# Modulation of the K blocks in four chunks due at their first K tile, the gate root's chain kept together on VectorE, and the first product of a block by operand parts, in a two-layer GLA/FoX trunk

## Chip, cores and metric

One core of a Trainium2 chip. The metric is the device time of one execution of the whole program in microseconds (us), median of three runs. One execution was also profiled; times inside the kernel come from its trace.

## The reference, cut to what matters

A two-layer decoder trunk on one sequence of 256 tokens and 2048 features, in float32. Every sub-layer is normalised, then scaled and shifted by columns that come from a conditioning vector `c`:

```python
mod = c_act @ w_mod[l] + b_mod[l]            # 6 sections of 2048: shift, scale, gate, twice
h = rmsnorm(x, norm_mix[l]) * (1 + scale_m) + shift_m
x = x + gate_m * mixer(h)                    # layer 0: GLA, layer 1: FoX
h = rmsnorm(x, norm_ffn[l]) * (1 + scale_f) + shift_f
x = x + gate_f * conv_ffn(h)

# GLA mixer
proj = h @ w_in                              # 2048 x 6160: q, k (1024 each), v, r (2048 each), a (16)
log_alpha = log_sigmoid(a @ w_gate + b_gate) / 16
o = chunked_linear_attention(q, k, v, log_alpha)
o = rmsnorm(o, g_norm) * silu(r)             # the norm is over each head of 512 columns
return o @ w_out
```

`c_act` is the activated conditioning vector. The tolerance asks for nearly full float32 products.

## The kernel before, in words

**Products.** Activations stand transposed (features on the 128 partitions, tokens along the free dimension), so the input of a projection is 16 K tiles of 128 features x 256 tokens. Each float32 operand is split into a high part and a rest. A weight tile of 128x1024 is cast on ScalarE to `wh` (line 125) and its rest `wl = w - wh` is formed on VectorE (line 129). A product then is three matmuls for each 128 columns, high x high (line 621), high x rest (line 622), rest x high (line 623), so 24 matmuls with 256 moving columns for one weight tile. In this text such a weight tile with its 24 matmuls is a **use**; they are numbered in the order in which their loads are issued, use 1 being the first tile of `q`. `wh` and `wl` each have four buffers, taken in turn, so the cast for use n+4 waits for the last matmul of use n.

**K blocks.** The first projection (GLA's `w_in`) doesn't wait for all of `h`. Its 16 K tiles are cut into three blocks, `BLOCKS = (4, 5, 7)`: K tiles 0 to 3, 4 to 8, 9 to 15. In a block the sections q, k, v0, v1, r0, r1 are swept in turn (one use for each K tile), then the 16 narrow columns `a`; in the last block `a` stands behind q. Block 1 is uses 1 to 24 and 25 (`a`), block 2 uses 26 to 55 and 56 (`a`), block 3 uses 57 to 63 (q), 64 (`a`) and 65 to 99. Sums of earlier blocks are copied back into PSUM by ScalarE (line 609). From use 100 on `w_out` follows.

**Modulation.** The columns `sc_m` and `sh_m` of K tiles 0 to 3 (the head) are made at the start on TensorE: eight early loads of 1 MB of `w_mod` and eight sums of eight matmuls (line 1270), with five filling matmuls behind some of them (line 1308, `KEEP = 5`). Those of the other K tiles are accumulated on VectorE by outer products: a step loads two tiles of 128 rows of `w_mod` in one DMA and does a scalar-times-tensor addition for each (line 273 for the first of a section, then line 275) on a tile `acc` as wide as the block has columns: 640 columns for block 2, 896 for block 3, 32 additions for each. When a section's last step is through, VectorE transposes and reduces `acc` into `red` (lines 285 and 286), TensorE closes the sum over partitions with a 128x20 or 128x28 matmul (line 302), and VectorE adds the bias and writes the columns (lines 318, 322). `tick()`, called at each use, hands out these steps at a pace; before the first use of a block a hook (`hooks[end - 1] = drain_bg`) does all that is left. Later sections (for the gate of layer 0 and for the FFN) are accumulated in the same manner with 1024 columns.

**h.** `make_h` makes for each K tile `hn = x * r` (line 527, VectorE), `h hi` with scale and shift (line 528, ScalarE), the same once more in float32 (line 530 on VectorE for K tiles 0 to 2 of a projection, else line 532 on ScalarE), and the rest `h lo` (line 533, VectorE).

**GLA's gate norm.** For each pair of heads `rsqrt` (lines 403 to 416) forms 1/sqrt by a start value and Newton steps: 13 small VectorE instructions on 128x4 numbers, each reading what the one before wrote. Its result is spread by a diagonal `dg` (line 422) and a TensorE matmul with ones (line 424).

**Order.** Each engine executes its own list of instructions strictly in the order in which a scheduler has put them when the kernel is built; `issue_after` gives it an additional edge. What stands on VectorE in one list is thus `wl`, `acc`, the reductions, `h`, the chain of the gate norm and more. SyncE issues all weight loads, also in order.

## Time and profile before

| | |
|---|---|
| device time, median of 3 runs | 2445.64 us (2445.29 to 2446.72) |
| the profiled execution's own time | 2444.97 us |
| its span in the trace | 2443.3 us |
| TensorE busy (matmuls) | 2388.1 us, 98% |
| VectorE busy | 1901.7 us, 78% |
| ScalarE busy | 1326.6 us, 54% |
| HBM read over the span | 260 GB/s |

Busy times are of the trace; matmuls are pipelined, so the busy time of one matmul (0.28 us in the rows) is longer than the distance between the starts of two. "a <- b" behind an idle time says that the instruction waited for the event b. `PEclk` is the TensorE clock as a share of full speed.

### The profile page before, as it was taken

Reading aid. Unit: us, or ns where it says so; the run is one execution under the profiler, and the core shown is the slowest. Engines: PE = TensorE matmul, PEld = TensorE weight load, DVE = VectorE, ACT = ScalarE, POOL = GpSimd, SP = SyncE. Lnnn points to the kernel's source line nnn. Section 1 sums busy time; section 2 is a strip of 40 time slices with the busy share of each in tenths; the row PEclk is TensorE's granted clock in tenths of the full one; section 3 lists DMA queues with packets and bytes.
Section 4 is the critical chain, followed back from the end, with each engine's and each line's share of the span. In section 5 each row is a group of like instructions: output and inputs, shape, how many; then the busy total and the mean of one; then the engine's idle time right before and its main releaser. Section 6 shows DMA issues by size and latency. Waiting matters only on the chain.

```text
span 2443.3 us, 46907 instructions
## 1 busy us (share of the span) xinstructions
PE 2388.1 (98%) x19089; PEld 2292.1 (94%) x19093; DVE 1901.7 (78%) x2548; ACT 1326.6 (54%) x1819; POOL 16.1 (1%) x35
## 2 busy tenths in 40 slices
PE   7999998999999999999999999999999999999998
PEld 5898898999999999999988888999999999999998
DVE  5887878887689999987577998887776777777544
ACT  4666864544656556543464555554755555555433
POOL 0000000000000000000000000000000000000000
PEclk9999998999999999999999999999999999999999
DMA  9997877899668999899589887686777777756553
GB/s 377 328 338 240 288 249 274 288 322 322 181 191 278 314 302 313 315 327 322 168 291 314 298 288 244 210 300 234 232 232 234 234 233 235 232 193 220 192 190 104
DMA packets 188293, 638.31 MB, mean 261 GB/s; under 512 B 23849, under 2 KB 24859, under 8 KB 187692
## 3 DMA queue, kind: packets, MB, share of 16 engines
q1 hardware_dynamic: 187112, 634.12, 77.2%
q8 instruction: 149, 2.44, 0.4%
q10 hardware_dynamic: 964, 1.20, 0.1%
q14 instruction: 68, 0.56, 0.1%
HBM read 633.14 MB, written 2.10 MB: 260 GB/s over the span
## 4 chain that ended last, share of the span: by engine, by line
PE 95%; DVE 2%; ACT 2%; DMA 1%; issue 1%; SPq 0%; DVEq 0%; ACTq 0%
PE pa L622 25%; PE pa L623 25%; PE pa L621 25%; PE pa L668 5%; PE pa L669 5%; PE pa L667 5%; DVE wl L129 1%; DMA wm<-in_w_mod_dram 1%; PE pe L1270 0%; DVE acc L275 0%; ACT wh L125 0%; PE pm L483 0%; PE pm L877 0%; DMA xtok<-in_x_dram 0%; PE pm L1088 0%
## 5 line engine op out<-in xcount | busy, mean ns | idle before, releaser
L125 ACT CAST wh<-w 128x1024 fp32r<-128x1024 f32 x820 | 857.4, 1048 | 965.7 <-PE pa L622 735.3
L129 DVE TENSOR_TENSOR wl<-w,wh 128x1024 fp32r<-128x1024 f32 x820 | 996.5, 1217 | 438.8 <-ACT wh L125 428.6
L622 PE MATMUL pa<-h,wh 128*128 128x256 f32 x3584 | 993.7, 278 | 13.3 <-DVE h L533 13.3
L621 PE MATMUL pa<-h,wh 128*128 128x256 f32 x3584 | 991.6, 278 | 2.2 <-ACT h L528 1.3
L623 PE MATMUL pa<-h,wl 128*128 128x256 f32 x3584 | 991.0, 278 | 1.7 <-DVE wl L129 1.7
L622 PEld LDWEIGHTS pa<-h,wh 128*128 128x128 f32 x3584 | 677.4, 189 | 15.1 <-DVE h L533 14.8
L621 PEld LDWEIGHTS pa<-h,wh 128*128 128x128 f32 x3584 | 675.3, 189 | 5.4 <-issue 1.5
L623 PEld LDWEIGHTS pa<-h,wl 128*128 128x128 f32 x3584 | 675.6, 189 | 2.0 <-DVE wl L129 1.9
L622 PE MATMUL pa<-op,wh 128*128 128x256 f32 x1920 | 529.4, 277 | 1.8 <-DVE op L549 1.8
L621 PE MATMUL pa<-op,wh 128*128 128x256 f32 x1920 | 528.9, 278 | 0.4 <-ACT op L548 0.2
L623 PE MATMUL pa<-op,wl 128*128 128x256 f32 x1920 | 524.8, 277 | 0.0
L275 DVE SCALAR_TENSOR_TENSOR acc<-wm,cT,acc 128x1024 f32<-128x1024 f32 (+2 forms) x360 | 444.3, 1235 | 10.7 <-DMA wm<-in_w_mod_dram 9.4
L622 PEld LDWEIGHTS pa<-op,wh 128*128 128x128 f32 x1920 | 362.0, 189 | 2.3 <-DVE op L549 2.3
L621 PEld LDWEIGHTS pa<-op,wh 128*128 128x128 f32 x1920 | 361.2, 189 | 1.1 <-ACT r L750 0.6
L623 PEld LDWEIGHTS pa<-op,wl 128*128 128x128 f32 x1920 | 359.2, 189 | 0.0
L668 PE MATMUL pa<-wh,h 128*128 128x512 f32 x512 | 200.2, 392 | 0.0
L667 PE MATMUL pa<-wh,h 128*128 128x512 f32 x512 | 198.8, 391 | 0.0
L669 PE MATMUL pa<-wl,h 128*128 128x512 f32 x512 | 194.4, 392 | 0.0
L669 PEld LDWEIGHTS pa<-wl,h 128*128 128x128 f32 x512 | 96.0, 188 | 19.7 <-DVE wl L129 0.3
L667 PEld LDWEIGHTS pa<-wh,h 128*128 128x128 f32 x512 | 96.1, 188 | 19.4
L668 PEld LDWEIGHTS pa<-wh,h 128*128 128x128 f32 x512 | 96.1, 188 | 19.2
L1140 ACT ACTIVATE y<-u,cw 128x256 f32<-128x256 f32 x176 | 101.6, 599 | 6.7 <-DVE act L1156 4.1
(264 smaller groups left out, 1351.3 us busy)
## 6 DMA issues: line engine op xcount, KB each, us to landing
wm<-in_w_mod_dram SPq DMA_DIRECT2D x320, 512.0 KB, 5.2
w<-in_ffn_w_up_dram SPq DMA_DIRECT2D x320, 512.0 KB, 4.5
w<-in_ffn_w_down_dram SPq DMA_DIRECT2D x176, 512.0 KB, 4.5
w<-in_fox_w_in_dram SPq DMA_DIRECT2D x128, 512.0 KB, 5.1
w<-in_gla_w_in_dram SPq DMA_DIRECT2D x96, 512.0 KB, 5.8
w<-in_gla_w_out_dram SPq DMA_DIRECT2D x32, 512.0 KB, 5.9
w<-in_ffn_w_up_dram SPq DMA_DIRECT2D x64, 256.0 KB, 4.0
w<-in_fox_w_out_dram SPq DMA_DIRECT2D x32, 512.0 KB, 5.9
```

The costliest lines, as they stand in the source:

```text
L125: nc.scalar.copy(out=hi, in_=src)
L129: order["v"] = nc.vector.tensor_tensor(out=lo, in0=src, in1=hi.bitcast(F32), op=ALU.subtract).ins
L275: nc.vector.scalar_tensor_tensor(out=st["a"], in0=wt[:, j, :], scalar=col, in1=st["a"], op0=ALU.mult, op1=ALU.add)
L621: nc.tensor.matmul(o, wh[:, ms], rh, start=(first and m % 2 == 0), stop=False, skip_group_check=True)
L622: nc.tensor.matmul(o, wh[:, ms], rl, start=False, stop=False, skip_group_check=True)
L623: nc.tensor.matmul(o, wl[:, ms], rh, start=False, stop=last, skip_group_check=True)
L667: nc.tensor.matmul(o, lh[:, ts_], wh[:, hs_], start=first, stop=False, skip_group_check=True)
L668: nc.tensor.matmul(o, ll[:, ts_], wh[:, hs_], start=False, stop=False, skip_group_check=True)
L669: nc.tensor.matmul(o, lh[:, ts_], wl[:, hs_], start=False, stop=last, skip_group_check=True)
L1140: nc.scalar.activation(y, u, AF.Identity, scale=cw[:, l * 3 + 2, r:r + 1], bias=cw[:, 6 + l, r:r + 1])
```

## The change

1. **Chunks.** The modulation of K tiles 4 to 15 is queued at the first use in four chunks, `MARKS = (4, 7, 9, 13, 16)`: K tiles 4-6, 7-8, 9-12, 13-15, that is 384, 256, 512 and 384 columns, each for scale and for shift. A step is now four tiles of 128 rows of `w_mod` (eight for 256 columns) in one DMA, with an addition for each; the DMAs are 28 instead of 32, of the same bytes in all, with rows of 1 to 2 KB instead of 2.5 and 3.5. All steps are handed out at one pace over block 1 and 2; if a chunk isn't complete when `h` asks for its first K tile, the rest is done there and its closing matmul comes at once (`flush_resting(True)`).
2. **Start.** The first three of the eight early sums stand ahead of the token sum on TensorE; three fillers instead of five; K tile 0's `h` comes ahead of the second and third weight split.
3. **Chain.** Each `wl`, and each `acc` addition but a section's first, is put behind the last instruction of the newest `rsqrt` chain (as of the last `tick`), so that the chain's 13 instructions stand together. `scale_of(0)` and `normalise(0)`, `normalise(1)` are queued earlier, and the paces of the side work and of the steps behind it change.
4. **First product of a block by operand parts.** The first weight tile that meets a fresh `h` does all high x high matmuls first, then all high x rest, then all rest x high.
5. The second modulation is on VectorE for the first four K tiles behind each of 0, 4, 9 in layer 0's mixer, and for the first five of every other `h`. The look-ahead of the weight loads is 2 until use 50 instead of 20; `SLOAD` is 100 instead of 48.

```diff
-NEAR = 20
+NEAR = 50
-KEEP = 5
+KEEP = 3
+MARKS = (4, 7, 9, 13, 16)
+EARLY = 3
-BG0, BG1 = 0.95, 0.75
+BG0, BG1 = 0.95, 0.95
...
             if after is not None:
                 es.enter_context(tc.issue_after(after))
+            es.enter_context(behind_chain())
             order["v"] = nc.vector.tensor_tensor(out=lo, in0=src, in1=hi.bitcast(F32), op=ALU.subtract).ins
...
-                        nc.vector.scalar_tensor_tensor(out=st["a"], in0=wt[:, j, :], scalar=col, in1=st["a"],
-                                                       op0=ALU.mult, op1=ALU.add)
+                        with behind_chain():
+                            nc.vector.scalar_tensor_tensor(out=st["a"], in0=wt[:, j, :], scalar=col, in1=st["a"],
+                                                           op0=ALU.mult, op1=ALU.add)
...
+    def behind_chain():
+        return tc.issue_after(chain["on"]) if chain["on"] is not None else ExitStack()
...
-            if m < 3:
-                nc.vector.tensor_scalar(out=t, in0=t, scalar1=sc, scalar2=sh, op0=ALU.mult, op1=ALU.add)
-            else:
-                nc.scalar.activation(t, t, AF.Identity, scale=sc, bias=sh)
+                if m - (max(b for b in STARTS if b <= m) if (l, kind) == (0, "m") else 1) < 4:
+                    nc.vector.tensor_scalar(out=t, in0=t, scalar1=sc, scalar2=sh, op0=ALU.mult, op1=ALU.add)
+                else:
+                    nc.scalar.activation(t, t, AF.Identity, scale=sc, bias=sh)
...
+        def by_part(ms, args):
+            edge = None
+            for n_ in range(3):
+                with ExitStack() as es:
+                    if edge is not None:
+                        es.enter_context(tc.issue_after(edge))
+                    for m in ms:
+                        last_ = mms(m, *args, n_)
+                    edge = last_
...
-        side.extend((apply(0), scores(2), apply(1), scores(3)))
+        side.extend((apply(0), scores(2), apply(1), scores(3), scale_of(0)))
         fold("v1", piece("v1", kts, off["v1"]))
         drain_side()
-        side.extend((apply(2), apply(3), scale_of(0), scale_of(2), normalise(0), normalise(1), normalise(2), normalise(3)))
+        side.extend((normalise(0), normalise(1), apply(2), apply(3), scale_of(2), normalise(2), normalise(3)))
...
     def staged_h(m):
-        if m in STARTS[:-2]:
-            n_ = STARTS.index(m) + 1
-            for key in ("sc_m", "sh_m"):
-                queue(mod_tasks(0, key, STARTS[n_] * P, BLOCKS[n_] * P, wide=True))
-            n_use = 6 * BLOCKS[n_ - 1]
-            set_pace(n_use - EASE)
-            end = fetched["use"] + n_use + (m > 0)
-            hooks[end - 1] = drain_bg
-            hooks[end] = lambda: h(STARTS[n_])
+        if m == 0:
+            for m0, m1 in zip(MARKS, MARKS[1:]):
+                for key in ("sc_m", "sh_m"):
+                    queue(mod_tasks(0, key, m0 * P, (m1 - m0) * P, wide=True))
+                need[m0] = len(bg)
+            pace["bg"] = len(bg) / float(6 * MARKS[2] + 2)
+            use = 6 * MARKS[0]
+            hooks[use] = lambda: h(MARKS[0])
+            hooks[use + 3] = lambda: h(MARKS[1])
+            use = 6 * MARKS[2] + 1
+            hooks[use] = lambda: h(MARKS[2])
+            hooks[use + 4] = lambda: h(MARKS[3])
+        if m in need:
+            while steps_done[0] < need[m]:
+                bg_step()
+            flush_resting(True)
         return first_h(m)
```

What this does to the lists of the engines is shown at three places. The first is VectorE where block 1 ends; before, `wl_1026` is the rest of `a` (use 25), `wl_1065` and `wl_1101` those of uses 26 and 27, and `acc_733` the second section of block 2:

```order
L275 SCALAR_TENSOR_TENSOR acc_733<-wm_875,cT,acc_733 128x640 x2
L129 TENSOR_TENSOR wl_996<-w_943,wh_995 128x1024
L129 TENSOR_TENSOR wl_1026<-w_984,wh_1025 128x176
L275 SCALAR_TENSOR_TENSOR acc_733<-wm_939,cT,acc_733 128x640 x2
L129 TENSOR_TENSOR wl_1065<-w_987,wh_1064 128x1024
L285 STREAM_TRANSPOSE mt_1056<-acc_733 128x512
L285 STREAM_TRANSPOSE mt_1059<-acc_733 128x128
L286 TENSOR_REDUCE red_1055<-mt_1056 128x16
L286 TENSOR_REDUCE red_1055<-mt_1059 128x4
L129 TENSOR_TENSOR wl_1101<-w_989,wh_1100 128x1024
L318 TENSOR_TENSOR mod<-pm_1092,bm 32x5 x4
```

The same place after; `wl_1184` is the rest of use 28, `wl_1213` that of use 29, and `acc_908` and `acc_1070` are scale and shift of K tiles 7 and 8:

```order
L132 TENSOR_TENSOR wl_1184<-w_1111,wh_1183 128x1024
L279 SCALAR_TENSOR_TENSOR acc_1070<-wm_870,cT,acc_1070 128x256
L290 TENSOR_REDUCE red_987<-mt_988 128x8
L279 SCALAR_TENSOR_TENSOR acc_1070<-wm_870,cT,acc_1070 128x256
L279 SCALAR_TENSOR_TENSOR acc_1070<-wm_947,cT,acc_1070 128x256
L322 TENSOR_TENSOR mod<-pm_1063,bm 32x2 x4
L279 SCALAR_TENSOR_TENSOR acc_1070<-wm_947,cT,acc_1070 128x256
L326 SCALAR_TENSOR_TENSOR mod<-mod,vec 128x2
L279 SCALAR_TENSOR_TENSOR acc_1070<-wm_947,cT,acc_1070 128x256 x6
L289 STREAM_TRANSPOSE mt_1150<-acc_1070 128x256
L290 TENSOR_REDUCE red_1149<-mt_1150 128x8
L132 TENSOR_TENSOR wl_1213<-w_1181,wh_1212 128x1024
```

The last two additions of block 2's sections stood two uses ahead of the boundary; now ten of the narrower ones stand behind the rest of use 28, inside block 2. On TensorE the matmul that reads `red_1149` stands behind the 72 products of uses 26 to 28 and ahead of `a` (use 25), which before came first.

The second place is VectorE where block 2 ends. Before, `acc_1675` is the second section of block 3, `wl_2061` and `wl_2097` the rests of uses 57 and 58:

```order
L129 TENSOR_TENSOR wl_2022<-w_1850,wh_2021 128x192
L275 SCALAR_TENSOR_TENSOR acc_1675<-wm_1846,cT,acc_1675 128x896
L590 MEMSET w_2144 128x112
L275 SCALAR_TENSOR_TENSOR acc_1675<-wm_1881,cT,acc_1675 128x896
L129 TENSOR_TENSOR wl_2061<-w_1883,wh_2060 128x1024
L275 SCALAR_TENSOR_TENSOR acc_1675<-wm_1881,cT,acc_1675 128x896
L129 TENSOR_TENSOR wl_2097<-w_1915,wh_2096 128x1024
L285 STREAM_TRANSPOSE mt_2052<-acc_1675 128x512
L285 STREAM_TRANSPOSE mt_2055<-acc_1675 128x384
L286 TENSOR_REDUCE red_2051<-mt_2052 128x16
L286 TENSOR_REDUCE red_2051<-mt_2055 128x12
```

After, `acc_2035` is the shift of K tiles 13 to 15, `wl_2384` and `wl_2417` the rests of uses 63 and 64, and `acc_2358` the next section, of 1024 columns:

```order
L132 TENSOR_TENSOR wl_2384<-w_2160,wh_2383 128x1024
L276 TENSOR_SCALAR acc_2358<-wm_2254,cT 128x1024
L279 SCALAR_TENSOR_TENSOR acc_2035<-wm_1999,cT,acc_2035 128x384
L132 TENSOR_TENSOR wl_2417<-w_2214,wh_2416 128x224
L279 SCALAR_TENSOR_TENSOR acc_2358<-wm_2256,cT,acc_2358 128x1024
L279 SCALAR_TENSOR_TENSOR acc_2035<-wm_2094,cT,acc_2035 128x384 x4
L279 SCALAR_TENSOR_TENSOR acc_2358<-wm_2356,cT,acc_2358 128x1024
L289 STREAM_TRANSPOSE mt_2323<-acc_2035 128x384
L290 TENSOR_REDUCE red_2322<-mt_2323 128x12
L322 TENSOR_TENSOR mod<-pm_2360,bm 32x3 x4
```

Six additions now stand between the rest of use 64 and the reduction. On TensorE the matmul that reads `red_2322` stands directly behind use 60.

The third place is VectorE at the second chain of the gate norm. Before (lines 410 to 416 are the chain's, `wl_4111` and `wl_4215` rests of uses 108 and 111):

```order
L414 TENSOR_TENSOR grs<-rt_3530,grs 128x4
L275 SCALAR_TENSOR_TENSOR acc_3700<-wm_3992,cT,acc_3700 128x1024
L129 TENSOR_TENSOR wl_4111<-w_3926,wh_4110 128x1024
L410 TENSOR_TENSOR rt_3530<-rv_3529,grs 128x4
L275 SCALAR_TENSOR_TENSOR acc_3700<-wm_4031,cT,acc_3700 128x1024
L129 TENSOR_TENSOR wl_4147<-w_3962,wh_4146 128x1024
L411 TENSOR_TENSOR rt_3530<-rt_3530,grs 128x4
L275 SCALAR_TENSOR_TENSOR acc_3700<-wm_4067,cT,acc_3700 128x1024
L129 TENSOR_TENSOR wl_4180<-w_4001,wh_4179 128x1024
L416 SCALAR_TENSOR_TENSOR grs<-rt_3530,grs 128x4
...
L422 TENSOR_SCALAR dg_3703<-ident,grs 128x128
```

After, at the second chain (`wl_3733` is the rest of use 96, `pm_3625` the closing matmul of the squares on TensorE):

```order
L964 COPY pvar<-pm_3625 128x2
L415 TENSOR_SCALAR rv_3662<-pvar 128x4
...
L422 TENSOR_TENSOR rt_3663<-rv_3662,grs 128x4
L423 TENSOR_TENSOR rt_3663<-rt_3663,grs 128x4
L428 SCALAR_TENSOR_TENSOR grs<-rt_3663,grs 128x4
L279 SCALAR_TENSOR_TENSOR acc_2992<-wm_3602,cT,acc_2992 128x1024
L132 TENSOR_TENSOR wl_3733<-w_3474,wh_3732 128x1024
L435 TENSOR_SCALAR dg_3711<-ident,grs 128x128
```

The chain's 13 instructions stand together, and the next `acc` addition and the next `wl` behind them. The first chain stands in the same way between `pvar<-pm_3257` ahead of it and `acc` and the rest of use 88 behind it.

More of the change, by code (lines that the diff above doesn't have):

```diff
@@ L94 @@
     cnt = [0]
-    order = {"v": None, "f": None}
+    order = {"v": None, "f": None, "w": None}
     def nm(s):
@@ L363, in tick @@
     def tick():
-        prefetch(PEND)
+        prefetch(min(PEND, fetched["use"] // 2 + 1))
+        chain["on"] = chain["new"]
         flush_resting()
@@ L434, in fetch_x, with load_x @@
         return xs
-    def load_x(xs):
+    def load_x(xs, between):
         for m in range(0, KT, 2):
@@ L445, in load_x @@
         half_sum()
-        token_sum(ss["t"][:, 0, :], True, True)
+        with tc.issue_after(between()):
+            token_sum(ss["t"][:, 0, :], True, True)
     ss = {}
@@ L620, in mms @@
             o = ps[m // 2][:, m % 2, :]
-            nc.tensor.matmul(o, wh[:, ms], rh, start=(first and m % 2 == 0), stop=False, skip_group_check=True)
-            nc.tensor.matmul(o, wh[:, ms], rl, start=False, stop=False, skip_group_check=True)
-            nc.tensor.matmul(o, wl[:, ms], rh, start=False, stop=last, skip_group_check=True)
+            for i, (w_, r_) in enumerate(((wh, rh), (wh, rl), (wl, rh))):
+                if n_ is None or n_ == i:
+                    mm = nc.tensor.matmul(o, w_[:, ms], r_, start=(first and i == 0 and m % 2 == 0),
+                                          stop=last and i == 2, skip_group_check=True)
+            return mm.ins
+        def by_part(ms, args):
+            edge = None
+            for n_ in range(3):
+                with ExitStack() as es:
+                    if edge is not None:
[3 more added lines that the diff above has]
+                    edge = last_
         for k in kts:
@@ L640, in stream_a @@
                         mms(m, *args)
+            elif fresh["h"]:
+                fresh["h"] = False
+                by_part(range(8), (k, wh, wl, rh, rl))
             else:
@@ L1292, with first_sums @@
         early_load(*args)
-    load_x(xs)
+    def first_sums():
+        with tc.issue_after(order["x"]):
+            for args in todo[:EARLY]:
+                last_ = early_sum(*args)
+        return last_
+    load_x(xs, first_sums)
     with tc.issue_after(order["s"]):
```

47 lines of the change are left out of this document (36 added, 11 removed).

## The prediction

> **What bounds the kernel now.** First the page's busy times and the chain of waits that ended last.
>
> ```profile
> PE 2388.1 (98%) x19089; PEld 2292.1 (94%) x19093; DVE 1901.7 (78%) x2548; ACT 1326.6 (54%) x1819; POOL 16.1 (1%) x35
> PE 95%; DVE 2%; ACT 2%; DMA 1%; issue 1%; SPq 0%; DVEq 0%; ACTq 0%
> ```
>
> TensorE (PE) sets the time nearly everywhere. So only two things count: what PE waits for, and how long it runs at a lower clock behind a wait. PE's waits, from the view of waits:
>
> ```profile
> PE pa L622 <- DVE h L533: 13.3, 7, 5.4
> PE pm L424 <- DVE dg L422: 8.3, 1, 8.3
> PE pm L483 <- DVE ss L476: 4.0, 1, 4.0
> PE pa L623 <- DVE wl L129: 1.7, 1, 1.7
> PE pm L302 <- DVE red L286: 1.7, 1, 1.7
> ```
>
> The change works on these. The windows around them (columns: time, busy time and instructions of PE, of the weight loads, of VectorE, ScalarE, GpSimd, then PE's clock, DMA share, GB/s):
>
> ```profile
> 100.00:110.00 10.00, 10.00 (x90) 10.00 (x90) 9.21 (x15) 4.62 (x7) 0.00 (x0) 1.00 0.69 209
> 110.00:120.00 10.00, 4.58 (x26) 4.26 (x25) 5.76 (x13) 9.97 (x20) 0.00 (x0) 0.78 1.00 380
> 120.00:130.00 10.00, 10.00 (x80) 10.00 (x80) 6.46 (x9) 3.66 (x4) 0.00 (x0) 0.88 0.68 214
> 200.00:210.00 10.00, 5.54 (x36) 5.05 (x35) 7.12 (x14) 9.49 (x18) 0.23 (x2) 0.83 0.38 107
> 210.00:220.00 10.00, 10.00 (x74) 10.00 (x75) 7.21 (x13) 5.82 (x10) 0.00 (x0) 0.83 0.40 112
> 380.00:390.00 10.00, 4.08 (x37) 3.89 (x35) 8.89 (x12) 2.10 (x2) 0.00 (x0) 0.93 1.03 410
> 390.00:400.00 10.00, 5.74 (x22) 4.86 (x23) 7.09 (x13) 3.78 (x18) 0.00 (x0) 0.50 0.55 213
> 400.00:410.00 10.00, 10.00 (x66) 10.00 (x66) 6.46 (x11) 3.33 (x4) 0.00 (x0) 0.72 0.26 77
> ```
>
> Undisturbed, PE does 90 matmuls in 10 us. What a window lacks of 90 is lost time, waits and low clock together: boundary 1 (110 to 130) 64 + 10 = 74 matmuls, 8.2 us; boundary 2 (200 to 220) 54 + 16 = 70, 7.8 us; the gate norm (380 to 410) 53 + 68 + 24 = 145, 16.1 us, of which I take off 2.5 for slower small matmuls that are in it anyway (estimate): 13.6. That is all the change could win there.
>
> What a use costs each engine, from the groups by form between 42 and 420 us, two casts that wait for PE, and PE's matmuls at the low clock:
>
> ```profile
> 106.70 1.05 ACT L125 CAST wh<-w 128x1024 fp32r<-128x1024 f32 x1 [1.67 <-PE pa L622]
> 109.42 1.05 ACT L125 CAST wh<-w 128x1024 fp32r<-128x1024 f32 x1 [1.67 <-PE pa L622]
> L129 DVE TENSOR_TENSOR wl<-w,wh 128x1024 fp32r<-128x1024 f32 x113 | 137.3, 1221 | 47.3 <-ACT wh L125 42.4 <-PE pm L424 3.2 <-PE pa L623 1.1
> L275 DVE SCALAR_TENSOR_TENSOR acc<-wm,cT,acc 128x1024 f32<-128x1024 f32 x47 | 60.1, 1278 | 7.4 <-DMA wm<-in_w_mod_dram 7.1
> L275 DVE SCALAR_TENSOR_TENSOR acc<-wm,cT,acc 128x896 f32<-128x896 f32 x30 | 34.3, 1142 | 0.2
> L275 DVE SCALAR_TENSOR_TENSOR acc<-wm,cT,acc 128x640 f32<-128x640 f32 x30 | 26.3, 880 | 0.4
> L129 DVE TENSOR_TENSOR wl<-w,wh 128x224 fp32r<-128x224 f32 x1 | 0.4, 386 | 0.0
> L285 DVE STREAM_TRANSPOSE mt<-acc 128x384 f32<-128x384 f32 x2 | 1.1, 538 | 0.0
> L286 DVE TENSOR_REDUCE red<-mt 128x12 f32<-128x384 f32 x2 | 1.1, 542 | 0.0
> 120.13 0.41 PE L621 MATMUL pa<-h,wh 128*128 128x256 f32 x1
> 120.34 0.41 PE L622 MATMUL pa<-h,wh 128*128 128x256 f32 x1
> ```
>
> A use is 2.72 us of PE (109.42 - 106.70). An addition costs 0.880 us at 640 columns, 1.278 at 1024: 0.22 us and 1.04 us for each 1000 columns. So 384 columns are 0.61 us, 256 are 0.48, 512 are 0.75 (worked out, not in the trace). At the low clock matmuls start every 0.21 us (120.34 - 120.13) instead of every 0.11 (10 us through 90). The clock columns 0.78 and 0.88 of the windows at boundary 1 mean some 6.8 us at half clock (2 x 10 x 0.22 + 2 x 10 x 0.12); PE works in 5.2 of them and so loses 2.6. I use that for each stall.
>
> **The change part by part.** *Start.*
>
> ```profile
> 2.19 17.25 SPq L248 DMA_DIRECT2D wm<-in_w_mod_dram  x8
> wm<-in_w_mod_dram SPq DMA_DIRECT2D x8, 1024.0 KB, 11.2
> 34.56 1.06 PE L1270 MATMUL pe<-wm,cz 128*32 128x512 f32 x8
> 38.07 1.58 ACT L528 ACTIVATE h<-hn,mod 128x256 fp32r<-128x256 f32 x3
> 38.72 0.74 PE L621 MATMUL pa<-h,wh 128*128 128x256 f32 x4 [1.34 <-ACT h L528]
> ```
>
> The eighth early load is issued by 19.44 us and lands some 11.2 later, 30.6; its sum begins only at 34.56, because PE does the token sum (a wait of 4.0 us), fillers and seven other sums first. With three sums ahead of the token sum and fewer fillers the last sum ends at about 31.7 at best, limited by the load. That is 35.62 - 31.7 = 3.9 us; `h` ahead of a cast of 1.05 us gives up to 1 more, of which I count 0.6: **-4.5 us** (bounds -5.5 and, if the load lands later because three more tiles are asked for, -1.5).
>
> *Boundary 1.* What PE waited for at 111.5 (h lo, 5.4 us) is gone, since K tiles 4 to 6 are ready before. But K tiles 7 and 8 are due three uses later, and their last ten 256-column additions stand behind the rest of use 28, whose cast waits for the end of use 24 (four buffers). From there: cast 1.05, `wl` 1.22, ten additions 4.8, a transpose and two reductions of 256 columns 1.2 (estimated from those of 384), small writes 0.8, in all some 9.1 us, less what the starts overlap (0.4). PE has 72 products in that time, 8.2 us: it waits 0.5 to 0.9 at the closing matmul. What is queued behind that matmul on PE is everything, `a` and all of uses 29 on. Then comes `a`, and use 29's cast waits for its end: three casts of 1.05 stand one behind the other before PE's next product (use 31's), 3.2 us; two `wl` later cost 1.6 and 1.3 more (the `aT` copy, an `hn` and 512-column additions lie between). If VectorE comes to use 24 with a lead of only 62.5 us of work against 65.3 of PE, uses 26 and 28 wait up to 3 us as well. The waits are 6.6 to 7, or some 10 with the poor lead; with the low clock behind that is 9.3 to 12.6, and I take 11.5, nearer to the poor lead, because VectorE has 20 us more to do in these blocks (next part): against 8.2 **+3.3** (bounds 0 and +5).
>
> *Block 2.* The work on VectorE up to use 56's rest, summed by its rows and these durations, is 160.8 us after use 1's rest, before 140.5:
>
> ```profile
> 40.81:109.00 68.19, 66.92 (x472) 63.14 (x473) 61.70 (x79) 36.40 (x48) 0.00 (x0) 0.95 0.94 346
> 109.00:203.00 94.00, 87.06 (x621) 81.81 (x619) 78.79 (x94) 63.63 (x95) 0.00 (x0) 0.96 0.89 318
> ```
>
> VectorE was busy 61.70 + 78.79 = 140.5 of 162 us. 128 additions in place of 64 pay the 0.22 us of each twice (14 us); the rest are second modulations moved from ScalarE and further small writes. The DMAs are 28 for 32 on SP's queue, the bytes the same. From use 30 to 54 that is 71.5 us against 24 x 2.72 = 65.3 of PE, so VectorE, which had room, is level with PE or behind. I count 0 here and take the lateness where it ends, at boundary 2; bounds 0 and +5.
>
> *Boundary 2.* The closing matmul that reads the last chunk's `red` stands on PE directly behind use 60. On VectorE the reduction stands behind use 64's rest, which waits for use 60's buffers, and six additions: 0.39 (224 columns wide, by its group) + 1.28 + 4 x 0.61 + 1.28 + 0.54 + 0.54 = 6.5 us in which PE has nothing. Then four small writes, h hi and h lo for K tile 13, some 0.65 + 0.6 + 0.9 and the ways between the engines, of which `a`'s 12 matmuls (1.4 us) cover the half: 1.4 more (estimate). Low clock behind: 2.6. Sum 10.5 against 7.8: **+2.7** (bounds -2, if use 64's rest is there earlier, and +5).
>
> *Gate norm.* The two chains in the trace, the first one's first and last instruction and two of the second's last four:
>
> ```profile
> 329.91 0.17 DVE L403 TENSOR_SCALAR rv<-pvar 128x4 f32<-128x4 f32 x1
> 333.72 0.16 DVE L416 SCALAR_TENSOR_TENSOR grs<-rt,grs 128x4 f32<-128x4 f32 x1
> 382.44 0.15 DVE L411 TENSOR_TENSOR rt<-rt,grs 128x4 f32<-128x4 f32 x1
> 391.81 0.15 DVE L416 SCALAR_TENSOR_TENSOR grs<-rt,grs 128x4 f32<-128x4 f32 x1
> ```
>
> The first ran nearly unbroken (3.97 us from the first start to the last end with one `wl` of 1.22 inside, so 2.8 alone) and cost PE nothing. The second was drawn out by `wl` and `acc` and cost 8.3. Now both stand together, and with that both stand, 2.8 us, an addition of 1.28 and 1.22, **ahead of the rest that PE needs next**: 5.3 us for use 88 and as much for use 96, counted from the closing matmul of the squares on PE, less the small score products beside it (1.8 at use 88, none at use 96): 3.5 and 5.3. The matmuls that read the squares wait for VectorE too: 1.0 + 2.2 at the first, 0.9 at the second. Low clock behind each, 2.6 twice. Sum 18.1 against 13.6: **+4.5** (bounds -6, if the first chain costs as little as before and only the second counts, and +6). Elsewhere (first products by parts in later sublayers, five second modulations on VectorE, FoX's chains) I take **-0.5** (bounds -4 and +3): the waits for h lo beyond boundaries 1 and 2 are 13.3 - 5.4 - 2.8 = 5.1 us at most, of the row of L533 above and this one:
>
> ```profile
> 209.88 0.39 PE L622 MATMUL pa<-h,wh 128*128 128x256 f32 x1 [2.78 <-DVE h L533]
> 203.16 0.41 PE L302 MATMUL pm<-red,quad 128*128 128x28 f32 x2 [1.68 <-DVE red L286]
> 204.32 0.41 PE L692 MATMUL pm<-h,wh 128*128 128x256 f32 x1
> ```
>
> Sum: -4.5 + 3.3 + 2.7 + 4.5 - 0.5 = +5.5. The profiled execution took 2444.97 us, 0.7 under the median; from the median 2445.64 it is 2451.1.
>
> The last two rows are also the ground for the low clock: a wait of 1.68 us, and 1.2 us later matmuls take 0.41. The Trainium skill, "TensorE: Matmul & The Clock Gate", section "Part 1: The HAM clock gate", says that the clock halves after at least one idle window of about 3.4 us of PE. The trace has it behind half of that; by the rule the sum would be +0.3 instead of +5.5 (rivals, below), and I go by the rows.
>
> **The rivals.** *The stalls go* (faster). VectorE runs ahead, so that the sums and chains are through before PE comes to them. For it: VectorE is idle a fifth of the time, and before, the first chain cost nothing. Against it: the order of rows and four buffers. It decides at use 60 and use 88: if the closing matmul there waits under 2 us, boundary 1 costs 4, boundary 2 costs 3 and the gate 7 instead of 8.2, 7.8 and 13.6, so -15.6 - 4.5 - 0.5 = -20.6: 2425. *Short waits leave the clock up.* The stalls at boundary 1 and at use 88 are made up of single waits of 3.5 us and less. Without 2.6 us behind each of the two the sum is +0.3: 2446, no change. The row at 204.32 speaks against. The Trainium skill's section named above would have it so. *The loads come late* (slower still). The look-ahead of 2 goes on until use 50, and the chunks' loads have rows of 1 to 2 KB where 2.5 and 3.5 stood. In block 1 the DMA share is 0.94 at 346 GB/s; if PE waits 0.3 us at each of 30 uses: +9 on the sum, 2460. *It doesn't do what it says*: the list shows the chains together and the chunks in place, so I give that nothing.
>
> **How the numbers follow.** Forecast 0.56, the stalls go 0.28, clock stays up 0.08, late loads 0.08. 0.2% of this kernel, 4.9 us, is about what a measurement can tell from no change. Inside the forecast the bounds reach from about -4 to +14, so of 0.56 I put 0.38 over +4.9, 0.16 within, 0.02 below. Faster: 0.28 + 0.02 = 0.30; same 0.16 + 0.08 = 0.24; slower 0.38 + 0.08 = 0.46. The forecast's own range is 2442 to 2460. The range for 8 in 10 reaches into the first rival: 2430 to 2461.
>
> **What would show it.** Right: the first product before 35 us; a PE wait for `red` of about 6.5 us near 200 us; waits for `wl` of 3 us and more at both chains; VectorE busy over 90% between use 30 and 60. Wrong: no wait over 2 us between 100 and 220 us, or PE's clock full through 300 to 400.

## The result and the profile after

| | before | changed |
|---|---|---|
| device time, median | 2445.47 us (2442.87 to 2446.72, 4 runs) | 2457.06 us (2456.01 to 2459.43, 4 runs) |
| ratio to before, 95% interval | | 1.0050 [1.0033, 1.0068] |
| profiled execution, its span | 2444.97, 2443.3 us | 2457.0, 2455.3 us |

The changed kernel is slower by 11.6 us, 0.5%; 2451 had been forecast, with a range of 2430 to 2461. First the page's busy times and the view of PE's waits, after (columns: total, times, longest; lines 650 and 717 are the products, 306 the closing matmul of a modulation section, 497 a token sum, 963 the matmul that reads the gate norm's squares):

```profile
PE 2388.3 (97%) x19095; PEld 2288.8 (93%) x19095; DVE 1921.5 (78%) x2645; ACT 1314.1 (54%) x1804; POOL 19.6 (1%) x35
PE pa L650 <- DVE wl L132: 13.5, 8, 5.2
PE pm L306 <- DVE red L290: 9.6, 2, 8.3
PE pa L650 <- DVE h L551: 4.9, 3, 2.3
PE pa L717 <- DVE wl L132: 4.3, 3, 2.4
PE pm L497 <- DVE ss L490: 4.0, 2, 2.7
PE pm L963 <- DVE gsq L960: 2.8, 2, 2.0
PE pm L437 <- DVE dg L435: 0.5, 1, 0.5
```

PE's busy time is as before (2388.1). Its large old waits have shrunk: h lo from 13.3 to 4.9 us, `dg` from 8.3 to 0.5. In their place stand waits for weight rests (1.7 before, 17.8 now) and for `red` (1.7 before, 9.6 now): VectorE is waited for in both kernels, for another product of its list. Behind 31 us no wait of PE is for a load and only one, of 0.5 us, for a cast, so the rival "the loads come late" did not come.

To see where the 12.0 us of span come from, take moments that both traces have, each an instruction that runs when PE has come to a certain place. Before (the cast that waits for the end of use 24 stands at 109.42 in a row above; then the first of GLA's gate columns, the first residual of `w_out`, the FFN's norm, the first operand of layer 1's output product):

```profile
248.09 1.23 DVE L722 SCALAR_TENSOR_TENSOR la<-la,le 128x1024 f32<-128x1024 f32 x1
463.37 0.88 DVE L700 SCALAR_TENSOR_TENSOR xT<-pa,mod,xT 128x256 f32<-128x256 f32 x2 [0.87 <-PE pa L623]
471.14 0.42 DVE L494 SCALAR_TENSOR_TENSOR ra<-pm,rb 128x256 f32<-128x256 f32 x1 [1.79 <-ACT rb L492]
1567.84 0.69 DVE L549 TENSOR_TENSOR op<-oTf,op 128x512 fp32r<-128x512 f32 x1 [0.61 <-ACT op L548]
```

The same after:

```profile
105.35 1.05 ACT L127 CAST wh<-w 128x1024 fp32r<-128x1024 f32 x1 [2.30 <-PE pa L650]
252.26 1.22 DVE L770 SCALAR_TENSOR_TENSOR la<-la,le 128x1024 f32<-128x1024 f32 x1
468.19 0.48 DVE L748 SCALAR_TENSOR_TENSOR xT<-pa,mod,xT 128x256 f32<-128x256 f32 x1 [0.31 <-PE pa L650]
478.91 0.42 DVE L508 SCALAR_TENSOR_TENSOR ra<-pm,rb 128x256 f32<-128x256 f32 x1 [4.71 <-ACT rb L506]
1579.86 0.69 DVE L575 TENSOR_TENSOR op<-oTf,op 128x512 fp32r<-128x512 f32 x1 [0.61 <-ACT op L574]
```

The differences are -4.1, +4.2, +4.8, +7.8 and +12.0 us. So the start gains 4.1 up to the end of use 24, the K blocks lose 8.3 behind that, the gate norm 0.6, the way from `w_out` into the FFN 3.0, and layer 1's mixer 4.2; nothing behind it differs.

Now the windows of the changed kernel at the places of the forecast (columns as in the prediction):

```profile
100.00:110.00 10.00, 7.78 (x63) 7.19 (x62) 10.00 (x23) 4.02 (x5) 0.00 (x0) 1.00 0.27 107
110.00:120.00 10.00, 6.84 (x58) 6.44 (x56) 9.61 (x25) 6.09 (x10) 0.00 (x0) 1.00 0.51 178
120.00:130.00 10.00, 7.61 (x60) 7.00 (x60) 9.85 (x19) 3.58 (x5) 0.00 (x0) 1.00 0.66 243
210.00:220.00 10.00, 4.63 (x41) 4.43 (x40) 9.72 (x14) 2.09 (x3) 0.00 (x0) 0.92 0.90 304
220.00:230.00 10.00, 7.10 (x39) 7.13 (x40) 4.23 (x10) 3.06 (x6) 0.23 (x2) 0.57 0.46 167
320.00:330.00 10.00, 7.97 (x96) 7.52 (x98) 3.94 (x19) 3.05 (x7) 0.64 (x3) 0.88 0.01 2
330.00:340.00 10.00, 7.99 (x74) 7.81 (x73) 9.94 (x13) 2.58 (x3) 0.43 (x1) 0.95 0.71 241
360.00:370.00 10.00, 4.83 (x34) 4.75 (x33) 7.92 (x23) 4.81 (x8) 0.00 (x0) 0.76 0.22 69
```

At boundary 1 VectorE is busy 29.5 of 30 us (10.00 + 9.61 + 9.85), and PE lacks 27 + 32 + 30 = 89 matmuls of 270, 9.9 us (8.2 before). At boundary 2 it lacks 49 + 51 = 100, 11.1 us (7.8 before). At the gate norm VectorE is idle 6 us of 320 to 330 and the loads stand nearly still (2 GB/s): the edges hold additions and rests back until the first chain has run, up to 330 us. The rows of the second chain show the same pattern; below them are PE's waits at the two chains:

```profile
362.65 0.17 DVE L415 TENSOR_SCALAR rv<-pvar 128x4 f32<-128x4 f32 x1
365.04 0.16 DVE L428 SCALAR_TENSOR_TENSOR grs<-rt,grs 128x4 f32<-128x4 f32 x1
365.12 1.28 DVE L279 SCALAR_TENSOR_TENSOR acc<-wm,cT,acc 128x1024 f32<-128x1024 f32 x1
366.31 1.22 DVE L132 TENSOR_TENSOR wl<-w,wh 128x1024 fp32r<-128x1024 f32 x1
```

```profile
332.52 0.39 PE L650 MATMUL pa<-h,wl 128*128 128x256 f32 x1 [2.01 <-DVE wl L132]
367.58 0.58 PE L650 MATMUL pa<-h,wl 128*128 128x256 f32 x1 [5.17 <-DVE wl L132]
```

The second chain takes 2.55 us together; the addition and the rest of use 96 follow, and PE's product begins 0.05 us after that rest ends, having waited 5.17 us.

### The profile page after: what moved, and what is told of

Same layout as the page of the kernel before. It is cut to its first block, busy times and chain, and to the rows that moved or that the text cites. A ratio compares the mean times of both kernels' runs of the same rounds, so it can differ in the third digit from the quotient of the medians.

```text
span 2455.3 us, 46997 instructions
## 1 busy us (share of the span) xinstructions
PE 2388.3 (97%) x19095; PEld 2288.8 (93%) x19095; DVE 1921.5 (78%) x2645; ACT 1314.1 (54%) x1804; POOL 19.6 (1%) x35
## 4 chain that ended last, share of the span: by engine, by line
issue 47%; PE 45%; DVE 4%; DMA 2%; ACT 1%; POOL 0%; SPq 0%; DVEq 0%; POOLq 0%; ACTq 0%
PE pa L650 39%; DVE acc L279 1%; DMA wm<-in_w_mod_dram 1%; DVE wl L132 1%; PE pa L717 1%; PE pa L715 1%; PE pa L716 1%; DMA w<-in_gla_w_in_dram 1%; ACT wh L127 0%; PE pm L1136 0%; PE pm L925 0%; DMA xtok<-in_x_dram 0%; PE pm L1100 0%; PE pm L1099 0%; PE pm L1127 0%
## 5 line engine op out<-in xcount | busy, mean ns | idle before, releaser
L650 PE MATMUL pa<-h,wh 128*128 128x256 f32 x7168 | 1230.5, 278 | 6.8 <-DVE h L551 4.9
L650 PEld LDWEIGHTS pa<-h,wh 128*128 128x128 f32 x7168 | 1079.4, 189 | 11.2 <-DVE h L551 5.7
L650 PE MATMUL pa<-h,wl 128*128 128x256 f32 x3584 | 975.7, 278 | 13.6 <-DVE wl L132 13.5
L650 PE MATMUL pa<-op,wh 128*128 128x256 f32 x3840 | 651.1, 276 | 0.7 <-ACT wh L127 0.5
L650 PEld LDWEIGHTS pa<-op,wh 128*128 128x128 f32 x3840 | 573.1, 188 | 1.1 <-ACT wh L127 0.7
L279 DVE SCALAR_TENSOR_TENSOR acc<-wm,cT,acc 128x1024 f32<-128x1024 f32 (+3 forms) x420 | 456.4, 1089 | 4.0 <-DMA wm<-in_w_mod_dram 2.1
L1191 DVE SCALAR_TENSOR_TENSOR y<-u,cw,y 128x254 f32<-128x254 f32 x176 | 83.1, 479 | 2.8
L1189 DVE SCALAR_TENSOR_TENSOR y<-u,cw,y 128x255 f32<-128x255 f32 x176 | 84.0, 477 | 0.0
L1210 ACT COPY u<-pa 128x512 f32<-128x512 f32 x88 | 49.8, 581 | 0.7
L542 ACT ACTIVATE h<-hn,mod 128x256 fp32r<-128x256 f32 x64 | 35.2, 594 | 14.0 <-DVE mod L322 9.5
## 6 DMA issues: line engine op xcount, KB each, us to landing
wm<-in_w_mod_dram SPq DMA_DIRECT2D x20, 1024.0 KB, 11.1
```

Source lines behind the costliest of these rows:

```text
L279: nc.vector.scalar_tensor_tensor(out=st["a"], in0=wt[:, j, :], scalar=col, in1=st["a"], op0=ALU.mult, op1=ALU.add)
L542: hot = nc.scalar.activation(hi, t, AF.Identity, scale=sc, bias=sh).ins
L650: mm = nc.tensor.matmul(o, w_[:, ms], r_, start=(first and i == 0 and m % 2 == 0), stop=last and i == 2, skip_group_check=True)
L1189: nc.vector.scalar_tensor_tensor(out=y[:, 1:], in0=u[:, :T - 1], scalar=cw[:, l * 3 + 1, r:r + 1], in1=y[:, 1:], op0=ALU.mult, op1=ALU.add)
L1191: nc.vector.scalar_tensor_tensor(out=y[:, 2:], in0=u[:, :T - 2], scalar=cw[:, l * 3, r:r + 1], in1=y[:, 2:], op0=ALU.mult, op1=ALU.add)
L1210: nc.scalar.copy(out=u[:, 2 * b:2 * b + 2, :], in_=ps[b])
```

## Experiments

All were timed beside runs of the kernel before on the same chip; the ratio is to those. The number that counts is the ratio, since the median of before moved between 2446.0 and 2446.6 us (2445.5 beside the changed kernel), so differences of medians across groups of runs can be off by about 1 us. Three groups: parts taken out of the change, parts put into the kernel before, and parts taken out of the best combination.

**Without the edges behind the chains** (1):

```diff
     def behind_chain():
-        return tc.issue_after(chain["on"]) if chain["on"] is not None else ExitStack()
+        return ExitStack()
```

> The changed kernel without the edges that put each weight rest and each addition behind the newest chain; all else is kept. Theory (edges): they are the cause of the new waits at both chains of the gate norm, of the wait for a weight rest of 2.4 us in layer 1's mixer, and, since the stalled additions hold up the loads behind them, of the late token sum ahead of layer 0's FFN (2.7 us). Then layer 1's mixer gives back about 4 us and the FFN's start 3 to 5; the gate norm comes back to a second chain that is drawn out, about as dear as now (plus or minus 3). In all 2449 us, 2445 to 2453. Rival (work): those losses come from the additional second modulations on VectorE and the higher pace of the additions; then the edges don't matter outside the gate norm, and the time is 2455 to 2459.

Measured: 2439.3 us, ratio 0.9975 [0.9964, 0.9985]: 17.8 us under the changed kernel and faster than before. The edges theory holds, by more than it said (its interval began at 2445). One part of it did not come: the second chain is not drawn out again, it takes 5.4 us here (367.88 to 373.25 us) and PE doesn't wait for `dg`. In layer 1's mixer PE is busy throughout again; the chain begins at 1458.32 us here, and PE is busy 20.00 of 20 us from 1440 to 1460 too (changed kernel, then this one; then the changed kernel's rows of the chain there):

```profile
1460.00:1480.00 20.00, 16.06 (x74) 11.97 (x73) 13.75 (x39) 9.35 (x19) 3.68 (x2) 1.00 0.19 61
```

```profile
1460.00:1480.00 20.00, 20.00 (x96) 16.06 (x95) 16.84 (x40) 9.68 (x19) 0.97 (x2) 1.00 0.71 240
```

```profile
1470.56 0.17 DVE L415 TENSOR_SCALAR rv<-qvar 128x16 f32<-128x16 f32 x1
1473.51 1.28 DVE L279 SCALAR_TENSOR_TENSOR acc<-wm,cT,acc 128x1024 f32<-128x1024 f32 x1
1474.70 1.22 DVE L132 TENSOR_TENSOR wl<-w,wh 128x1024 fp32r<-128x1024 f32 x1
1475.97 1.19 PE L717 MATMUL pa<-wl,h 128*128 128x512 f32 x4 [2.45 <-DVE wl L132]
```

It is the gate norm's pattern again. And the FFN's token sum no longer waits for `ss`; the waits from 290 to 500 us that are left of this kernel are three, of 3.4 us for `op`, 2.3 for h lo and 2.0 for `gsq`.

**Edges for the gate norm's chains alone** (2): the last instruction of a chain becomes `chain["new"]` only where the chain has 4 columns.

```diff
-                chain["new"] = nc.vector.scalar_tensor_tensor(out=q, in0=t, scalar=1.5, in1=q, op0=ALU.subtract,
-                                                              op1=ALU.mult).ins
+                last_ = nc.vector.scalar_tensor_tensor(out=q, in0=t, scalar=1.5, in1=q, op0=ALU.subtract,
+                                                       op1=ALU.mult).ins
+                if nn == 4:
+                    chain["new"] = last_
```

> The changed kernel with the edges for the chains of the gate norm alone (4 columns), not for those of layer 1's mixer (16 columns). Theory (edges): only the loss in layer 1's mixer goes, 4 us: 2453 us, and the FFN's start keeps its wait of 2.7 us. Rival (work): no change, 2456 to 2458.

Measured: 2452.4 us, 1.0030 [1.0019, 1.0042], 4.7 us under the changed kernel, as the edges theory had it. The wait of 2.7 us for `ss` ahead of the FFN stays. So of the 17.8 us some 5 fall to layer 1's chains and 13 to the two of the gate norm with what follows from them.

**The old two blocks of modulation** (3): `staged_h` and the marks of the kernel before, everything else of the change.

```diff
-    h = lazy(staged_h, KT, 2, MARKS)
+    h = lazy(staged_h, KT, 2, STARTS)
```

> The changed kernel with the modulation of the K blocks as before (two blocks of 640 and 896 columns, what is left done at the end of a block); start, edges, second modulations and products by parts are kept. Theory (chunks): 64 wide additions instead of 128 narrow ones, and no closing matmul behind half-done chunks: of the 8 us that the trace of the change loses from use 25 to 65 some 7 go; 2449 to 2451 us. Rival (second modulations): VectorE's lateness there comes from the nine second modulations moved to it; then at most 2 us go, 2455 us or more.

Measured: 2447.9 us, 1.0014 [1.0005, 1.0023], 9.1 us under the changed kernel, a little more than the theory's 7. The eight waits for a weight rest between 100 and 290 us are gone; at each boundary one wait for `red`, of 4.9 us, is left.

**The start alone, on the kernel before** (4):

```diff
-        token_sum(ss["t"][:, 0, :], True, True)
+        with tc.issue_after(between()):
+            token_sum(ss["t"][:, 0, :], True, True)
...
+            if m == 0 and (l, kind) == (0, "m"):
+                with tc.issue_after(ins):
+                    split_to(1, 2)
+                    with tc.issue_after(hot):
+                        split_to(2, 2)
```

> The kernel before with the start of the change alone: three early sums ahead of the token sum, three fillers for five, K tile 0's h ahead of the second and third weight split. Theory: PE begins the first product 5 us earlier and nothing behind takes that back, 2440 to 2441 us. Rival: it runs into VectorE and the saturated loads in block 1, and half of it or more is given back at the first boundary, 2443 to 2445 us.

Measured: 2443.1 us, 0.9987 [0.9978, 0.9996]: 2.9 us, the rival's side. The first boundary takes part of it back. There PE arrives before VectorE has made the reduction and waits, where before it did not wait for `red`; the wait for h lo behind it is then 2.6 instead of 5.4 us. The row of its trace:

```profile
110.03 0.62 PE L303 MATMUL pm<-red,quad 128*128 128x20 f32 x2 [4.57 <-DVE red L287]
```

**The next section held back at boundary 2** (5):

```diff
-    pace["bg"] = BG0
+    pace["bg"], pace["acc"] = BG0, -8.0
     gla_rest(0, *args)
```

> The changed kernel with the next section's additions (1024 columns, for the gate of layer 0) held back by eight steps, so that none of them stands between use 64's rest and the last chunk's reduction at the second boundary. Theory (what stands in VectorE's list between the rest and the reduction is what PE waits for): the wait for red of 8.3 us falls by two additions of 1.28 and the 0.57 us of their load, to about 5.2, and the time to 2453 to 2454 us. Rival (VectorE is late as a whole, and the held additions are paid a few uses later): 2456 to 2458 us.

The two parts of the theory came apart. The rows of the changed kernel's list and its PE, then PE of this one, then this one's wait for the FFN's token sum:

```profile
215.75 0.39 DVE L132 TENSOR_TENSOR wl<-w,wh 128x224 fp32r<-128x224 f32 x1
216.06 3.77 DVE L279 SCALAR_TENSOR_TENSOR acc<-wm,cT,acc 128x1024 f32<-128x1024 f32 x5
220.40 1.28 DVE L279 SCALAR_TENSOR_TENSOR acc<-wm,cT,acc 128x1024 f32<-128x1024 f32 x1 [0.57 <-DMA wm<-in_w_mod_dram]
222.20 0.55 DVE L290 TENSOR_REDUCE red<-mt 128x12 f32<-128x384 f32 x1
222.90 0.57 PE L306 MATMUL pm<-red,quad 128*128 128x12 f32 x2 [8.27 <-DVE red L290]
```

```profile
215.66 0.57 PE L306 MATMUL pm<-red,quad 128*128 128x12 f32 x2 [4.57 <-DVE red L290]
```

```profile
PE pm L497 <- DVE ss L490: 6.0, 2, 4.8
```

The wait for `red` fell from 8.3 to 4.6 us, so what stands between rest and reduction is what PE waits for. But the time is 2456.9 us, 1.0042 [1.0029, 1.0054], no different from the changed kernel. By the moments of its trace it is 8.0 us ahead at the first `la` (244.30 us), 3.2 at the first residual of `w_out` (465.00) and 1.6 at the FFN's norm (477.35). So most is lost within `w_out`, where PE does 385 matmuls from 415 to 465 us (439 in the changed kernel), and some ahead of the FFN, where the wait for `ss` rose from 2.7 to 4.8 us. The rival was right on the total; that it is the held steps that are paid there is read from the order, no run took it apart.

**The edges alone, on the kernel before** (6): of part 3 of the change the edges, not the queue order.

```diff
+            es.enter_context(behind_chain())
             order["v"] = nc.vector.tensor_tensor(out=lo, in0=src, in1=hi.bitcast(F32), op=ALU.subtract).ins
...
+                        with behind_chain():
+                            nc.vector.scalar_tensor_tensor(out=st["a"], in0=wt[:, j, :], scalar=col, in1=st["a"],
+                                                           op0=ALU.mult, op1=ALU.add)
```

> The kernel before with the edges behind the chains alone. Theory (edges cost at every chain, whatever the rest): the wait of 8.3 us for dg goes, but waits for a weight rest of 3 to 6 us come at both chains of the gate norm, with a low clock behind, and layer 1's mixer loses 4 us: 2447 to 2452 us. Rival (the edges are good where the queue of side work is as before): the gate norm loses 8 us less and layer 1 nothing: 2437 to 2440 us.

Measured: 2445.5 us, 0.9997 [0.9988, 1.0006]: no change, between the two. Its waits (lines shifted: 632 and 678 products, 492 the token sum):

```profile
PE pm L492 <- DVE ss L485: 7.9, 2, 4.0
PE pa L632 <- DVE wl L130: 6.4, 2, 5.2
PE pa L678 <- DVE wl L130: 2.5, 1, 2.5
```

The trace is of a run of 2450.25 us, 4.8 over the median, so only the waits are read from it. The wait of 8.3 us for `dg` is gone; the second chain takes 2.55 us (348.46 to 351.01). Of the theory's new waits two are there, 5.2 for a rest at the second chain and 2.5 in layer 1's mixer, none at the first chain; one of 3.9 for the FFN's token sum comes to them. By the time, what goes and what comes cancel here.

**The gate norm's queue order and paces alone, on the kernel before** (7):

```diff
-GP0 = 0.8
-GP1 = 1.4
+GP0 = 0.9
+GP1 = 1.2
...
-BG0, BG1 = 0.95, 0.75
+BG0, BG1 = 0.95, 0.95
...
-        side.extend((apply(0), scores(2), apply(1), scores(3)))
+        side.extend((apply(0), scores(2), apply(1), scores(3), scale_of(0)))
...
-        side.extend((apply(2), apply(3), scale_of(0), scale_of(2), normalise(0), normalise(1), normalise(2), normalise(3)))
+        side.extend((normalise(0), normalise(1), apply(2), apply(3), scale_of(2), normalise(2), normalise(3)))
```

> The kernel before with only the order of the gate norm's side work and its paces as in the change (first chain queued earlier, its two normalisations ahead of the last two heads, second chain behind those; paces 0.9, 1.2, 0.95). Theory (this order, not the edges, mends the gate norm): the second chain stands ahead of the need for it, the wait of 8.3 us for dg goes, and a smaller one comes in its place: 2438 to 2441 us. Rival (without the edges the second chain is drawn out all the same): 2444 to 2447 us.

Measured: 2434.9 us, 0.9958 [0.9946, 0.9971], 11.6 us under before, more than the theory said. Order and paces were changed together, so the gain belongs to both. The first row of the second chain in the kernel before (its last is the row at 391.81 in the prediction), then the first and last of this kernel's, and PE's two waits at the gate norm:

```profile
354.53 0.16 DVE L403 TENSOR_SCALAR rv<-pvar 128x4 f32<-128x4 f32 x1
```

```profile
364.74 0.17 DVE L403 TENSOR_SCALAR rv<-pvar 128x4 f32<-128x4 f32 x1
371.02 0.16 DVE L416 SCALAR_TENSOR_TENSOR grs<-rt,grs 128x4 f32<-128x4 f32 x1
```

```profile
363.58 0.58 PE L915 MATMUL pm<-ones,gsq 128*128 128x1 f32 x4 [3.29 <-DVE gsq L912]
366.40 1.22 PE L621 MATMUL pa<-op,wh 128*128 128x256 f32 x4 [2.25 <-ACT op L548]
```

Without an edge the chain takes 6.4 us from end to end, with other work between, and nobody waits for it. It isn't earlier: it begins 10.2 us later than in the kernel before. There it took 37.4 us, and PE came to the matmul that reads `dg` 29.6 us behind the chain's start (at 384.1 us), so it waited; here that matmul stands 9.1 us behind the start (at 373.84 us), and 6.4 us fit. So the new order and paces bring the chain together without an edge. Why the scheduler then puts less between its instructions, no run shows.

**No edges and two blocks** (8): (1) and (3) together.

```diff
-        return tc.issue_after(chain["on"]) if chain["on"] is not None else ExitStack()
+        return ExitStack()
...
-    h = lazy(staged_h, KT, 2, MARKS)
+    h = lazy(staged_h, KT, 2, STARTS)
```

> The changed kernel without the edges and with the modulation in two blocks as before; kept are the start, the first product by parts, the second modulations, the side queue's order and the paces. Theory (edges and chunks cost apart from one another, 17.8 and 9.1 us): 2430 us, 2427 to 2434. Rival (part of what either loses is the same lateness of VectorE): 2436 to 2440 us.

Measured: 2430.1 us, 0.9939 [0.9927, 0.9952], the sum of the two, 16.5 us under before. Together with (11) it is the fastest kernel of the study. The changed look-ahead and `SLOAD` stay in it; no run takes them out alone.

**Two chunks in the change's own scheme, no edges** (9), against (1):

```diff
-MARKS = (4, 7, 9, 13, 16)
+MARKS = (4, 9, 16)
...
-            pace["bg"] = len(bg) / float(6 * MARKS[2] + 2)
+            pace["bg"] = len(bg) / float(6 * MARKS[1] + 2)
+            hooks[6 * MARKS[0]] = lambda: h(MARKS[0])
+            hooks[6 * MARKS[1] + 1] = lambda: h(MARKS[1])
```

> The changed kernel without the edges, with the change's own scheme of chunks (all queued at the first use, one pace, due at their first K tile) but two chunks of 640 and 896 columns instead of four: 64 wide additions instead of 128 narrow ones. With four chunks and no edges the time was 2439.3 us, with the old two blocks 2430.1. Theory (narrowness: 64 more instructions of 0.22 us fixed cost each make VectorE late): 2429 to 2433 us. Rival (the scheme, due times and one pace, makes the loss): 2437 to 2441 us.

Measured: 2433.5 us, 0.9948 [0.9936, 0.9961]; 0.5 us over the end of the theory's interval, 5.8 under the four chunks of (1). At the first of the gate columns (`la`, the moment used above) it is at 244.82 us by its trace, (1) at 250.57 and (8) at 246.14. So up to there the scheme is as good as the old one. Going from four chunks to two takes away 64 additions and also two of the four moments at which a chunk is due; that the number of additions is what costs is argued, this run doesn't tell the two apart. By the waits the gain is at the second boundary: 4.9 us for `red`, 7.5 in (1); at the first it is 7.8, and 7.7 for rests and `red` in (1). The 3.4 us to (8) come later and are not explained; the two intervals overlap.

**Second modulations as before, in (8)** (10):

```diff
-                if m - (max(b for b in STARTS if b <= m) if (l, kind) == (0, "m") else 1) < 4:
+                if m < 3:
```

> No edges, two blocks (2430.1 us), and the second modulation on VectorE for K tiles 0 to 2 of a projection only, as before. Theory (VectorE is the engine that is late, so each 0.4 us moved to it costs or does nothing): 2428 to 2431 us. Rival (with h behind ScalarE's casts and copies at the boundaries, the move is what mends the wait for h lo): 2433 to 2437 us.

Measured: 2433.4 us, 0.9950 [0.9938, 0.9963], 3.3 us more than (8); by the medians the rival, though the intervals of the two overlap ((8) ends at 0.9952). In its trace a wait of 2.4 us for h lo stands at the first boundary that (8) does not have, as the rival said.

**First product in the old order, in (8)** (11):

```diff
-                fresh["h"] = True
+                fresh["h"] = False
```

> No edges, two blocks (2430.1 us), and the first product of a block in the old order (high x high, high x rest, rest x high for each 128 columns). Theory (by parts, PE has 8 products to do while h lo and the weight rest are still made): 2431 to 2434 us without it. Rival (it is waited for all the same): 2429 to 2430.5 us.

Measured: 2431.1 us, 0.9938 [0.9925, 0.9950]: 1.0 us by the medians, not told apart from none.

**Start and queue order, on the kernel before** (12): the diff of (7) on the kernel of (4), with its paces:

```diff
-GP0 = 0.8
-GP1 = 1.4
+GP0 = 0.9
+GP1 = 1.2
```

> The kernel before with the start of the change and with the gate norm's side order and paces, nothing else. Theory (the two gains, 2.9 and 11.6 us, stand at different places and add up): 2431 to 2433 us. Rival (the start's gain is given back at the boundaries of the K blocks): 2434 to 2436 us.

Measured: 2433.1 us, 0.9944 [0.9931, 0.9958], 13.1 us under before, 0.1 over the theory's interval; 2.9 and 11.6 make 14.5, so the two add up but for 1.4 us, less than the intervals tell apart. Its interval overlaps that of (8): most of what (8) gains over the kernel before is the start and this order with its paces.

## Why the forecast came out, and where its steps failed

**Start, -4.5 us.** The trace gives -4.1 at the end of use 24, -2.9 where the start stands alone. The mechanism was right, the size nearly. Not as said: the last sum ended at 34.3, not 31.7, since the sum ahead of it waited 2.00 us for its load and the clock was then at half for 3.4 us (the last sum took 1.77 us, 1.06 before), and the first product began at 36.96, not before 35 us. That is 1.8 us earlier than before; the rest of the gain was made behind it. There before waited 1.9 us for h lo and the first rest (42.09 in its trace), and its clock was at half from 40.44 to 47.27 us; now 16 matmuls follow each other and half clock lasts from 37.42 to 40.83. The low clock at the start had no term in the sum.

**Boundary 1 and block 2, +3.3 and 0.** Together with boundary 2 this was +6.0; measured +8.3. By windows boundary 1 lost 1.7 more than before and boundary 2 3.3 more, which leaves some 3.3 for the stretches between and ahead, inside the bounds of 0 to 5 of which I took the lower end. At boundary 1 the waits were as described (rests of uses 26 to 28: 1.16, 0.72, 1.80; the closing matmul 1.36; later rests 1.42 and 0.90), 7.4 us of them, but the low clock of 2.6 us did not come: the clock column is 1.00 in all three windows. The three casts behind one another cost PE nothing of that size either: the trace has no wait for `wh` there, because the casts did not wait for the end of `a` (the cast of use 29 begins at 116.87 us, `a` at 120.03).

**Boundary 2, +2.7.** Right in its place and its rows: 6.5 us had been added up for the list from use 64's rest to the reduction, 8.27 were waited, 0.57 of it for a load. Experiment (5) shows the cause of the wait, and also that mending it there gives nothing by itself.

**Gate norm, +4.5.** This step was too dear by 3.9: by the two moments the place costs +0.6. Its waits came out near their prices: 0.8 and 2.0 for the squares (1.0 and 2.2 said, and 0.9 at the second chain, which did not come), 2.0 and 5.2 for the rests (3.5 and 5.3), in all 10.5 with the 0.5 for `dg` where 12.9 had been said; what is left falls to the low clock, which cost less than 5.2. The drawn-out second chain was rightly named as what cost 8.3 us: 37.4 us from end to end before, 2.55 in the changed kernel, 6.4 in (7), and only before is it waited for. What I had wrong is what mends it. I gave that to the edges; the order and paces of the side work, which had no term of their own, do it alone and are worth 11.6 us (7), and the edges take that back, 13 us with what follows at the FFN by (1) and (2).

**Elsewhere, -0.5 with bounds -4 and +3.** This step failed: +7.2, outside the bounds. I had counted only the waits for h lo that a trace of before shows. But the edges hold for every later chain as well, so layer 1's mixer, where before has no wait of more than 0.6 us, lost 4.2; (1) and (2) show that as their effect. The 3.0 at the FFN's start go with the edges at the gate norm. In the changed kernel ScalarE's casts from 440 to 480 us wait 12.8 us in all for loads of `w_out`, where before those of that stretch wait for PE alone, and the token sum then waits 2.7 us for `ss`. While an addition waits behind a chain its `wm` buffer isn't free, and SyncE's queue, in order, stands (2 GB/s at 320 to 330 us). SyncE's own waits for additions from 290 to 400 us, in the changed kernel and then in (1):

```profile
SPq L251 <- DVE acc L279: 56.8, 17, 22.8
```

```profile
SPq L251 <- DVE acc L279: 19.5, 20, 2.5
```

The longest is 14.8 to 23.2 us in each of the five kernels with the edges ((2), (3), (5) and (6) beside the changed one) and 2.5 us or less in each of those without, and a wait for `ss` ahead of the FFN stands in the first five alone. The loads are made up later: 410 GB/s from 460 to 470 us, 251 before. So that the edges hold up the loads and make the token sum late is shown; that the second follows from the first is read from the traces, no run took it apart.

**The low clock.** I charged 2.6 us to each stall. At boundary 1, with seven waits of 0.34 to 1.80 us, none of it came; "short waits leave the clock up" was right there and wrong at the two chains (0.88, 0.95 and 0.76), where waits of 2.0 and 5.2 stood. The last section shows what bears on it.

**The signs.** Of the four that would show the forecast right two came, a PE wait for `red` at boundary 2 (8.27 us, 6.5 said) and VectorE busy over 90% (85.4 of the 92 us from 122 to 214). The rests were waited for over 3 us at the second chain only (2.0 and 5.2), and the first product did not begin before 35 us. "The stalls go" was to show by closing matmuls that wait under 2 us at use 60 and use 88; they waited 8.27 and 2.0. Without the edges and the chunks, in (8), the time is 2430.1, near that rival's 2425.

**The total.** The direction was right, the size was not: +5.5 us had been added up and 12.0 came by the trace. Against the sum the start is 0.4 worse, the K blocks 2.3 worse, the gate norm 3.9 better and the rest 7.7 worse. That 2457 lies near 2451 is in part luck, since the gate norm's error covers half of that of the later chains and the FFN; it lies near the upper end of the forecast's own range of 2442 to 2460.

## What to carry to other kernels

An edge that keeps a latency-bound chain together also puts everything in order behind it: count the next instruction that the bounding engine needs, at every place where the same helper is used, and not only at the one that the trace shows as bad. A drawn-out chain costs what it ends late: 37.4 us against 29.6 us of room cost 8.3 here, while layer 1's chain in (1), 14 us from end to end (1458.32 to 1472.33), cost nothing. So compare its length with the room up to its reader first, and try the order and the paces of the queue, which brought it to 6.4 us, before an edge. And cutting accumulations narrower multiplies the fixed cost of an instruction: at 0.22 us, 64 more of them are an estimated 14 us on an engine that had little room, so chunk by what is due and not finer.
